# Feed-forward products with the high and low activations side by side in one moving operand of 512 columns

## Chip, cores and metric

The kernel runs on one core of one Trainium2 chip. The metric is the device time of one execution in microseconds; the number for the kernel before is the median of 3 runs.

## What is computed

Two transformer layers in float32 on 256 tokens of width 1024. Each ends in a feed-forward block: normalize, multiply by a 1024 x 4096 matrix, relu, square, multiply by a 4096 x 1024 matrix, add to the residual stream. The change touches these two blocks; attention, convolution and gates before them stay as they are.

```python
def rms_norm(x, g):
    xf = x.astype(jnp.float32)
    y = xf * lax.rsqrt(jnp.mean(xf * xf, axis=-1, keepdims=True) + EPS)
    return (y * g.astype(jnp.float32)).astype(x.dtype)

# end of the first layer (hybrid_layer); D_MODEL 1024, D_FF 4096, SEQ 256
    h = rms_norm(x, norm2_g)
    return x + jnp.square(jax.nn.relu(h @ w_up)) @ w_down
...
# end of the second layer (second_block)
        hf = _rmsnorm(h, norm_ffn_g[l]) @ w_ff1[l]
        h = h + jnp.square(jax.nn.relu(hf)) @ w_ff2[l]
    return _rmsnorm(h, norm_final_g)
```

## The kernel before

**Products.** A float32 operand is written as the sum of a high part, rounded to the type fp32r, and a low part, the remainder. A product is then high weights x high activations, high weights x low activations, and low weights x high activations (`mm3`, L258, its matmuls at L264, L266 and L268). Weights are the stationary operand (128 x 128), activations the moving one: 128 rows of one contraction tile k and all 256 tokens. A `Feat` (class at L270) is a group that makes four output tiles o of 128 features: its two PSUM tiles `ps[0]` and `ps[1]` (half b = 0 and 1) hold two output tiles of 256 columns each, one bank a half. The pool `psm` has four such banks, so two groups can be open at once.

**Order.** A unit of weights is 1 MB: four contraction tiles by four output tiles. `chunk(c)` takes the next unit and issues its 16 x 3 matmuls. In the last chunk of a group the matmuls of half 0 come first, then its eviction `evac`, then those of half 1, then its eviction; in the others both halves alternate. `prod` (L375) runs groups one behind the other, or two in turns (`pair`). TensorE's instructions run in the order of the program (it is in `MANUAL`). Those of ScalarE and VectorE are sorted before the run by a planner, which follows what it takes to be ready and, among ready ones, program order, lifted for side work.

**Weights.** `Stream.next` loads units ahead and splits the one that is needed two units later in two pieces: ScalarE rounds the high part (L123, 128 x 1024), VectorE subtracts for the low part (L126). A split needs buffers of a unit that is used up.

**The up product** (`ffn_up`): 8 groups g of 8 contraction tiles, so two units each; the first two groups are a pair. Eviction of a half: ScalarE takes the relu from PSUM (L929), VectorE squares in SBUF (L930), then `split_into` makes the high part on ScalarE (L396) and the low part on VectorE (L397) in a `Split`, where one tile holds high and low parts of two contraction tiles beside each other.

**The down product.** In the first layer it is `residual` with 32 contraction tiles: two Feat groups of eight units, one behind the other. Eviction: VectorE scales from PSUM (L867), adds to the residual stream x (L868), ScalarE squares it (L873), VectorE adds the squares up (L880, L882). `add_up` puts the column sums of the squares on TensorE (L436) one call of `pump` later, that is in the midst of the next group's first unit; the next normalization hangs on them. In the second layer the down product is a `Tok` group: activations stationary, weights moving, 512 columns (L355 to L357).

`pump` is called twice in each chunk and issues a piece of side work (normalization sums, transposes, the memory's loading).

Of the kernel before, what the change touches and what calls it, by code (L numbers as in the profile page):

```python
# [9 lines left out]
F32 = mybir.dt.float32  # L10
# [6 lines left out]
T = 256  # L17
# [38 lines left out]
class Split:  # L56
# [11 lines left out]

    def lo(self, k, n=1):
        return self._part(1, k, n)  # L70

    def _part(self, h, k, n):
        t = self.tiles[k // 2]
# [87 lines left out]
def hybrid_conformer_kernel(ctx, tc, stop, dbg, xT, memT, wall, wtok, wkiwi, wcmp, par_d, cst_d, gfin_d, out):  # L161
# [3 lines left out]
    const = ctx.enter_context(tc.tile_pool(name="const", bufs=1))  # L165
    half = ctx.enter_context(tc.tile_pool(name="half", bufs=H_BUFS))
    sm = ctx.enter_context(tc.tile_pool(name="sm", bufs=2))
    psm = ctx.enter_context(tc.tile_pool(name="psm", bufs=4, space=bass.MemoryType.PSUM))
    pss = ctx.enter_context(tc.tile_pool(name="pss", bufs=3, space=bass.MemoryType.PSUM))
    pso = ctx.enter_context(tc.tile_pool(name="pso", bufs=1, space=bass.MemoryType.PSUM))  # L170

# [19 lines left out]

    def PS(name="s"):
        return pss.tile([128, 512], F32, name=name, tag="s")

    def bc(ap, n):
        return ap.unsqueeze(1).to_broadcast([128, n, ap.shape[-1]])
# [18 lines left out]
    def v4(ap):  # L215
        return ap.rearrange("p n (s a) -> p n s a", s=2)
# [40 lines left out]

    ALL8 = list(range(8))  # L258

    def mm3(ps_ap, wh, wl, xh, xl, first, last, part=None):  # L260
        ps_ap = ps_ap.rearrange("p (a s) -> p a s", s=2)
        xh, xl = turns(xh), turns(xl)
        if part in (None, 0):
            P.matmul(out=ps_ap, lhsT=wh, rhs=xh, start=first, stop=False, skip_group_check=True)  # L264
        if part in (None, 1):
            P.matmul(out=ps_ap, lhsT=wh, rhs=xl, start=False, stop=False, skip_group_check=True)  # L266
        if part in (None, 2):
            P.matmul(out=ps_ap, lhsT=wl, rhs=xh, start=False, stop=last, skip_group_check=True)  # L268

    class Feat:  # L270


        def __init__(self, act, kts, evac, kmajor=False):
            self.act, self.kts, self.evac, self.kmajor = act, kts, evac, kmajor
            self.nch = len(kts) // 4
            self.ps = None

        def chunk(self, c):
            if self.ps is None:
                self.ps = [psm.tile([128, 2, T], F32, name="m", tag="m") for _ in range(2)]  # L280
            ps, act = self.ps, self.act
            wh, wl = W.next()
            wh = wh.rearrange("p (k o) -> p k o", k=4)
            if wl is not None:
                wl = wl.rearrange("p (k o) -> p k o", k=4)
            ks = self.kts[4 * c:4 * c + 4]
            end = c == self.nch - 1

            def one(kk, o, part=None):
                k = ks[kk]  # L290
                sl = slice(o * 128, o * 128 + 128)
                first = c == 0 and kk == 0 and o % 2 == 0
                last = end and kk == 3
                if wl is None:
                    P.matmul(out=plain(ps[o // 2])[:, o % 2], lhsT=wh[:, kk, sl], rhs=v3(act.raw(k)), start=first, stop=last, skip_group_check=True)  # L295
                else:
                    mm3(ps[o // 2][:, o % 2], wh[:, kk, sl], wl[:, kk, sl], act.hi(k), act.lo(k), first, last, part)

            if not end or self.kmajor:
                for kk in range(4):  # L300

                    for part in range(3) if self.kmajor and wl is not None else (None,):
                        for o in range(4):
                            one(kk, o, part)
                    if kk == 1:
                        pump()
                if end:
                    for b in range(2):
                        self.evac(plain(ps[b]), 2 * b, 2)
            else:  # L310
                for b in range(2):
                    for kk in range(4):
                        for o in (2 * b, 2 * b + 1):
                            one(kk, o)
                    self.evac(plain(ps[b]), 2 * b, 2)
                    if b == 0:
                        pump()
            pump()

    class Tok:  # L320
# [10 lines left out]
        def chunks(self, c, num, mid=None):  # L331

            if self.ps is None:
                self.ps = [psm.tile([128, 512], F32, name="m", tag="m") for _ in range(2)]
            ps, act, n = self.ps, self.act, self.n
            ws = []
            for _ in range(num):
# [44 lines left out]
                for c in range(g.nch):  # L382
                    g.chunk(c)

    def group(act, kts, evac, kmajor=False):
        prod([Feat(act, kts, evac, kmajor)])

    def tok_group(act, kts, n, evac):
        prod([Tok(act, kts, n, evac)])
# [93 lines left out]
    with tc.manual_schedule(engines=MANUAL):  # L483
# [3 lines left out]
        with tc.manual_schedule(engines={mybir.EngineType.Activation}):  # L487
            nc.scalar.dma_start(out=par0, in_=par_d[:, 0:8])
            A.activation(out=S([128, 1], "tab"), in_=ones[:, 0:1], func=AF.Exp)
        warm = psm.tile([128, 2, T], F32, name="m", tag="m")  # L490
        for i in range(WARM):
            P.matmul(out=warm[:, i % 2, 0:128], lhsT=ones, rhs=ones)
        x = B8(name="x")
# [361 lines left out]

        prod([ba(0), ba(1)])

        def residual(act, kts, x, sp, gname, scale_b=None, kmajor=False, pair=True, stats=None):

            def one(hf):  # L860
                def ev(ps, o, n):
# [25 lines left out]

                        later.append((STATS_LAG, add_up))

                return Feat(act, kts, ev, kmajor=kmajor and hf == 0)  # L890

            prod([one(0), one(1)], pair=pair)

# [4 lines left out]
        def ffn_up(act, src, tagr, bcast):  # L898
            res = {}

            def norm_side():
                for _ in range(9):
                    yield
                s = sq_sum(src, "s")
                for _ in range(5):
                    yield
                ps = col_stats(s)
                r = rstd_col(ps, D, "r" + tagr)
                r2 = const.tile([128, 2], F32, name="rsq" + tagr)
                V.tensor_tensor(r2, r, r, op=ALU.mult)  # L910
                res["col"] = r2
                if not bcast:
                    return
                dg = col_diag(r2)
                yield
                ps = diag_bcast(dg)
                rb = S([128, T], "rb", 4)
                A.activation(out=rb, in_=ps, func=AF.Copy)
                res["b"] = rb

            res["gen"] = start(norm_side())
            hs = Split([])
            gs = []
            for g in range(8):
                hs.tiles += HL("hh", 4).tiles

                def ev(ps, o, n, g=g):
                    r = S([128, 2, T], "pr", PR_BUFS)
                    A.activation(out=v4(r), in_=ps, func=AF.Relu)  # L929
                    V.tensor_tensor(r, r, r, op=ALU.mult)  # L930
                    split_into(hs, r, n, 4 * g + o)

                gs.append(Feat(act, ALL8, ev))
            prod(gs[:2], pair=True)
            prod(gs[2:])
            return hs, res
# [40 lines left out]
        mems, mem_steps, mem_sum = load_mem()  # L977
        msd = start(mem_side())
        st3 = {}
        residual(hs, list(range(32)), x, None, None, scale_b=res["b"], pair=False, stats=st3)  # L980
        drain(msd)
        dump2("x3", x)
        if stop == 1:
# [45 lines left out]
        def heads_pv(pt, nb, v, h0, sp, tt, pool=None):  # L1029

            if pool is psm:
                po = psm.tile([128, 2, T], F32, name="m", tag="m").rearrange("p a t -> p (a t)")
            else:
                po = PS() if pool is pss else pso.tile([128, 512], F32, name="o", tag="o")
            for r in range(2):
# [162 lines left out]
        for hf in range(2):  # L1198
# [19 lines left out]

            group(xs2, ALL8, ev_qi)
            kiwi = S([128, T], "rb", 4)  # L1220
            ps = psm.tile([128, 2, T], F32, name="m", tag="m")
            wh, wl = W.next()
            for k in range(8):
                sl = slice(128 * k, 128 * k + 128)
# [300 lines left out]
```

## Time and profile before

| | |
|---|---|
| median of 3 runs (lowest, highest) | 895.32 us (895.29, 895.41) |
| the profiled execution's own time, its span | 895.22 us, 893.4 us |
| TensorE matmuls, busy | 881.9 us, 99% of the span, 7240 instructions |
| VectorE | 659.8 us, 74% |
| ScalarE | 545.4 us, 61% |
| GpSimd | 18.6 us, 2% |
| HBM read | 162.58 MB, 183 GB/s over the span |

All numbers of the trace are of one profiled execution. A matmul's row is longer than its distance from the next, since matmuls overlap in the pipeline; the pace is read from start to start in the timeline. PE is TensorE's matmul, DVE VectorE, ACT ScalarE; L12 is line 12 of the kernel. In names like `m<-fh,wh` the output comes first; `m` are the accumulators of `psm`, `wh` and `wl` the high and low parts of the weights, `hh` the tiles of the up product's result (high and low), `fh` those of its input. In the first layer the up product takes 231 to 318 us and the down product 318 to 404.6 us; in the second layer they take 715.5 to 803.4 and 803.4 to 886.5 us.

### The profile page before, as it was taken

To read this page: it belongs to the slowest core of one execution; us is meant where nothing else is said; L and a number is where in the kernel's file an instruction comes from. 1 tells how busy PE (TensorE), PEld (TensorE's weight loads), DVE (VectorE), ACT (ScalarE), POOL (GpSimd) and SP (SyncE) were. 2 spreads that over 40 slices of the span, in tenths; PEclk is the share of its full clock that TensorE was granted. 3 is DMA by queue.
4 is the path that set the end of the run, shared out by engine and by line. 5 is a ranking of instruction groups with operands and counts; after the bars stand their busy time and mean duration, and the time that the engine had idled before them with its cause. 6 is when DMAs were issued, how large, how long until landed. Compare 5 with 4: busy or idle time off the path is not lost.

```text
span 893.4 us, 17269 instructions
## 1 busy us (share of the span) xinstructions
PE 881.9 (99%) x7240; PEld 852.8 (95%) x7240; DVE 659.8 (74%) x1037; ACT 545.4 (61%) x925; POOL 18.6 (2%) x21
## 2 busy tenths in 40 slices
PE   9999999999999999999999999999999999999996
PEld 8999999999999999999998989999999999998885
DVE  6678899457787675648699999997787777665542
ACT  7634667444575564434697799977566657554432
POOL 0121000000000000000000000000000000000000
PEclk9999999999999999999999999999999999999999
DMA  8944623455555566554553356354565265555531
GB/s 305 313 161 146 222 98 140 158 211 198 190 190 189 192 241 219 197 189 140 186 209 107 139 193 236 112 192 166 199 250 203 104 216 189 190 202 209 198 142 48
DMA packets 25566, 165.01 MB, mean 185 GB/s; under 512 B 2960, under 2 KB 3600, under 8 KB 6928
## 3 DMA queue, kind: packets, MB, share of 16 engines
q1 hardware_dynamic: 25056, 163.37, 51.8%
q8 instruction: 57, 0.93, 0.4%
q10 hardware_dynamic: 432, 0.53, 0.2%
q14 instruction: 21, 0.17, 0.1%
HBM read 162.58 MB, written 1.05 MB: 183 GB/s over the span
## 4 chain that ended last, share of the span: by engine, by line
PE 89%; DVE 5%; ACT 2%; issue 1%; DMA 1%; POOL 1%; POOLq 0%; DVEq 0%
PE m L264 23%; PE m L266 23%; PE m L268 23%; PE m L355 4%; PE m L356 4%; PE m L357 4%; DVE wl L126 2%; PE m L295 2%; DMA wr<-in_wall_dram 1%; PE m L352 1%; DVE y L1147 1%; PE o L785 1%; PE s L769 1%; PE s L1065 1%; POOL coqk L631 1%
## 5 line engine op out<-in xcount | busy, mean ns | idle before, releaser
L126 DVE TENSOR_TENSOR wl<-wr,wh 128x1024 fp32r<-128x1024 f32 (+2 forms) x300 | 350.4, 1191 | 155.2 <-ACT wh L123 154.8
L123 ACT ACTIVATE wh<-wr 128x1024 fp32r<-128x1024 f32 (+2 forms) x300 | 298.5, 1028 | 204.2 <-PE m L266 95.9
L264 PE MATMUL m<-xnh,wh 128*128 128x256 f32 x376 | 106.6, 283 | 0.0
L266 PE MATMUL m<-xnh,wh 128*128 128x256 f32 x376 | 103.4, 275 | 0.0
L268 PE MATMUL m<-xnh,wl 128*128 128x256 f32 x376 | 103.4, 275 | 0.0
L264 PE MATMUL m<-xh,wh 128*128 128x256 f32 x384 | 100.5, 282 | 0.9 <-ACT xh L523 0.9
L266 PE MATMUL m<-xh,wh 128*128 128x256 f32 x384 | 98.0, 276 | 0.0
L268 PE MATMUL m<-xh,wl 128*128 128x256 f32 x384 | 97.8, 275 | 0.0
L1146 ACT ACTIVATE cp<-u,par 128x255 f32<-128x255 f32 (+23 forms) x192 | 78.8, 492 | 0.0
L266 PEld LDWEIGHTS m<-xnh,wh 128*128 128x128 f32 x376 | 72.2, 192 | 0.7 <-issue 0.5
L264 PEld LDWEIGHTS m<-xnh,wh 128*128 128x128 f32 x376 | 72.2, 192 | 0.7 <-issue 0.5
L264 PEld LDWEIGHTS m<-xh,wh 128*128 128x128 f32 x384 | 69.8, 192 | 2.8 <-issue 1.4
L268 PEld LDWEIGHTS m<-xnh,wl 128*128 128x128 f32 x376 | 72.2, 192 | 0.0
L264 PE MATMUL m<-x5h,wh 128*128 128x256 f32 x256 | 70.8, 277 | 0.0
L264 PE MATMUL m<-fh,wh 128*128 128x256 f32 x256 | 70.6, 276 | 0.0
L264 PE MATMUL m<-hh,wh 128*128 128x256 f32 x256 | 70.6, 276 | 0.0
L268 PE MATMUL m<-x5h,wl 128*128 128x256 f32 x256 | 70.4, 275 | 0.0
L266 PE MATMUL m<-fh,wh 128*128 128x256 f32 x256 | 70.4, 275 | 0.0
L268 PE MATMUL m<-fh,wl 128*128 128x256 f32 x256 | 70.4, 275 | 0.0
L266 PE MATMUL m<-hh,wh 128*128 128x256 f32 x256 | 70.4, 275 | 0.0
L268 PE MATMUL m<-hh,wl 128*128 128x256 f32 x256 | 70.4, 275 | 0.0
L266 PE MATMUL m<-x5h,wh 128*128 128x256 f32 x256 | 70.4, 275 | 0.0
(380 smaller groups left out, 2318.1 us busy)
## 6 DMA issues: line engine op xcount, KB each, us to landing
wr<-in_wall_dram SPq DMA_DIRECT2D x145, 1024.0 KB, 4.9
wr<-in_wall_dram SPq DMA_DIRECT2D x4, 512.0 KB, 9.1
mem<-in_memT_dram SPq DMA_DIRECT2D x4, 512.0 KB, 5.8
wr<-in_wtok_dram SPq DMA_DIRECT2D x2, 560.0 KB, 5.5
wr<-in_wall_dram SPq DMA_DIRECT2D x4, 256.0 KB, 5.1
wck<-in_wcmp_dram SPq DMA_DIRECT2D x2, 512.0 KB, 8.6
cst<-in_cst_dram SPq DMA_DIRECT2D x1, 776.0 KB, 10.7
x<-in_xT_dram SPq DMA_DIRECT2D x2, 256.0 KB, 4.2
```

Source lines behind the costliest of these rows:

```text
L123: self.nc.scalar.activation(out=hi[:, sl], in_=raw[:, sl], func=AF.Copy)
L126: self.nc.vector.tensor_sub(lo[:, sl], raw[:, sl], hi[:, sl].bitcast(F32))
L264: P.matmul(out=ps_ap, lhsT=wh, rhs=xh, start=first, stop=False, skip_group_check=True)
L266: P.matmul(out=ps_ap, lhsT=wh, rhs=xl, start=False, stop=False, skip_group_check=True)
L268: P.matmul(out=ps_ap, lhsT=wl, rhs=xh, start=False, stop=last, skip_group_check=True)
L295: P.matmul(out=plain(ps[o // 2])[:, o % 2], lhsT=wh[:, kk, sl], rhs=v3(act.raw(k)), start=first, stop=last, skip_group_check=True)
L352: P.matmul(out=o.rearrange("p a s -> p s a"), lhsT=act.raw(k)[:, tk], rhs=wh[:, w], start=first, stop=last)
L355: P.matmul(out=o, lhsT=xh, rhs=wh[:, w], start=first, stop=False)
L356: P.matmul(out=o, lhsT=xh, rhs=wl[:, w], start=False, stop=False)
L357: P.matmul(out=o, lhsT=xl, rhs=wh[:, w], start=False, stop=last)
L631: G.tensor_tensor(co, ms, mhalf, op=ALU.pow)
L1146: A.activation(out=p[:, i, 0:T - d], in_=u[hf][:, i, 0:T - d], func=AF.Copy, scale=w[i])
```

## The change

In groups g = 2 to 7 of both up products and in both groups of the first layer's down product (`wide`), a contraction tile's high and low activations, which already lie in one tile, become one moving operand of 512 columns against the high weights; a second matmul of 256 columns multiplies low weights by high activations onto the first 256 of these. An output tile's accumulator is then a whole bank, the low activations' product in its second half. A PSUM tile of `psm` is now two banks and the pool has two of them (`PM`), so a wide half takes one tile, a wide group both; a group that isn't wide has both its halves in one tile. In a wide chunk all matmuls of half 0 come before those of half 1. The eviction of a wide half has ScalarE copy the second halves to SBUF and VectorE add the first halves to them; after that the old eviction goes on from SBUF, in the up product with relu and square as one VectorE instruction (max with 0, times itself).

```diff
+    def both(self, k):
+        return self.tiles[k // 2][:, :, k % 2]
...
-    psm = ctx.enter_context(tc.tile_pool(name="psm", bufs=4, space=bass.MemoryType.PSUM))
+    psm = ctx.enter_context(tc.tile_pool(name="psm", bufs=2, space=bass.MemoryType.PSUM))
...
+    def PM():
+
+        return psm.tile([128, 2, 2, T], F32, name="m", tag="m")
...
+    def mm2(ps_ap, wh, wl, xhl, first, last):
+
+        P.matmul(out=ps_ap.rearrange("p h (a s) -> p h a s", s=2), lhsT=wh, rhs=xhl.rearrange("p h (s a) -> p h a s", s=2),
+                 start=first, stop=False, skip_group_check=True)
+        P.matmul(out=ps_ap[:, 0].rearrange("p (a s) -> p a s", s=2), lhsT=wl, rhs=turns(xhl[:, 0]), start=False, stop=last,
+                 skip_group_check=True)
...
-        def __init__(self, act, kts, evac, kmajor=False):
-            self.act, self.kts, self.evac, self.kmajor = act, kts, evac, kmajor
+        def __init__(self, act, kts, evac, kmajor=False, wide=False):
+            self.act, self.kts, self.evac, self.kmajor, self.wide = act, kts, evac, kmajor, wide
...
+        def chunk_wide(self, c):
+
+            if self.ps is None:
+                self.ps = [None, None]
+            wh, wl = (w.rearrange("p (k o) -> p k o", k=4) for w in W.next())
+            ks = self.kts[4 * c:4 * c + 4]
+            end = c == self.nch - 1
+            for b in range(2):
+                if c == 0:
+                    self.ps[b] = PM()
+                m = self.ps[b]
+                for kk in range(4):
+                    for o in range(2):
+                        sl = slice((2 * b + o) * 128, (2 * b + o) * 128 + 128)
+                        mm2(m[:, o], wh[:, kk, sl], wl[:, kk, sl], self.act.both(ks[kk]), c == 0 and kk == 0, end and kk == 3)
+                if end:
+                    t = S([128, 2, T], "pr", PR_BUFS)
+                    A.activation(out=v4(t), in_=plain(m[:, :, 1]), func=AF.Copy)
+                    V.tensor_tensor(v4(t), plain(m[:, :, 0]), v4(t), op=ALU.add)
+                    self.evac(v4(t), 2 * b, 2)
+                pump()
+
         def chunk(self, c):
+            if self.wide:
+                self.chunk_wide(c)
+                return
             if self.ps is None:
-                self.ps = [psm.tile([128, 2, T], F32, name="m", tag="m") for _ in range(2)]
+                m = PM()
+                self.ps = [m[:, 0], m[:, 1]]
...
-        def residual(act, kts, x, sp, gname, scale_b=None, kmajor=False, pair=True, stats=None):
+        def residual(act, kts, x, sp, gname, scale_b=None, kmajor=False, pair=True, stats=None, wide=False):
...
-                    A.activation(out=v4(r), in_=ps, func=AF.Relu)
-                    V.tensor_tensor(r, r, r, op=ALU.mult)
+                    if g < 2:
+                        A.activation(out=v4(r), in_=ps, func=AF.Relu)
+                        V.tensor_tensor(r, r, r, op=ALU.mult)
+                    else:
+                        V.scalar_tensor_tensor(out=v4(r), in0=ps, scalar=0.0, in1=ps, op0=ALU.max, op1=ALU.mult)
                     split_into(hs, r, n, 4 * g + o)
 
-                gs.append(Feat(act, ALL8, ev))
+                gs.append(Feat(act, ALL8, ev, wide=g > 1))
...
-        residual(hs, list(range(32)), x, None, None, scale_b=res["b"], pair=False, stats=st3)
+        residual(hs, list(range(32)), x, None, None, scale_b=res["b"], pair=False, stats=st3, wide=True)
```

## Rows read from the trace of the kernel before

A timeline row is: start us, us, engine, line, operation, output<-input, shapes, count; in brackets how long the engine sat idle before it, and what released it.

**Rows 1.** Stages: start:end, length, then busy us (x instructions) of each engine

```profile
231.00:318.00 87.00, 87.00 (x781) 87.00 (x780) 61.77 (x76) 53.16 (x69) 1.08 (x1) 1.00 0.57 196
...
318.00:404.60 86.60, 86.60 (x778) 86.60 (x777) 49.89 (x57) 40.21 (x48) 0.70 (x1) 1.00 0.58 207
```

**Rows 2.** TensorE's waits over the whole run: us in total, times, longest

```profile
PE s L1164 <- DVE ys L1161: 1.1, 1, 1.1
...
PE s L436 <- ACT pr L873: 0.2, 1, 0.2
```

**Rows 3.** Timeline of TensorE, first down product, 256 columns; first and last of 38

```profile
359.78 0.28 PE L266 MATMUL m<-hh,wh 128*128 128x256 f32 x1
...
363.91 0.28 PE L268 MATMUL m<-hh,wl 128*128 128x256 f32 x1
```

**Rows 4.** Timeline of TensorE, second down product, 512 columns; first and last of 21

```profile
829.65 0.38 PE L356 MATMUL m<-wl,hh 128*128 128x512 f32 x1
...
833.97 0.38 PE L355 MATMUL m<-wh,hh 128*128 128x512 f32 x1
```

**Rows 5.** Timeline of TensorE, token product of 280 columns; first and last of 16

```profile
31.40 0.28 PE L356 MATMUL m<-wl,xh 128*128 128x280 f32 x1
...
33.19 0.28 PE L356 MATMUL m<-wl,xh 128*128 128x280 f32 x1
```

**Rows 6.** Timeline of ScalarE and VectorE, first up product, middle of a group

```profile
302.13 2.02 ACT L123 ACTIVATE wh<-wr 128x1024 fp32r<-128x1024 f32 x2 [1.77 <-PE m L266]
...
303.23 2.36 DVE L126 TENSOR_TENSOR wl<-wr,wh 128x1024 fp32r<-128x1024 f32 x2 [1.79 <-ACT wh L123]
...
305.56 0.69 DVE L930 TENSOR_TENSOR pr<-pr 128x512 f32<-128x512 f32 x1
...
306.28 0.63 ACT L396 ACTIVATE hh<-pr 128x512 fp32r<-128x512 f32 x1 [0.76 <-DVE pr L930]
```

**Rows 7.** Timeline of TensorE: the first matmul of a group, three boundaries

```profile
263.63 0.28 PE L264 MATMUL m<-fh,wh 128*128 128x256 f32 x1
...
275.16 0.36 PE L264 MATMUL m<-fh,wh 128*128 128x256 f32 x1
...
318.12 0.28 PE L264 MATMUL m<-hh,wh 128*128 128x256 f32 x1
```

**Rows 8.** Timeline of ScalarE at two of these boundaries

```profile
263.64 0.63 ACT L396 ACTIVATE hh<-pr 128x512 fp32r<-128x512 f32 x1 [1.89 <-DVE pr L930]
...
264.18 1.04 ACT L123 ACTIVATE wh<-wr 128x1024 fp32r<-128x1024 f32 x1
...
318.21 1.06 ACT L123 ACTIVATE wh<-wr 128x1024 fp32r<-128x1024 f32 x1 [0.58 <-PE m L266]
...
319.18 0.58 ACT L929 ACTIVATE pr<-m 128x512 f32<-128x512 f32 x1
```

**Rows 9.** Timeline of VectorE at the three boundaries

```profile
266.39 0.69 DVE L930 TENSOR_TENSOR pr<-pr 128x512 f32<-128x512 f32 x1
...
278.35 0.69 DVE L930 TENSOR_TENSOR pr<-pr 128x512 f32<-128x512 f32 x1
...
319.31 1.23 DVE L126 TENSOR_TENSOR wl<-wr,wh 128x1024 fp32r<-128x1024 f32 x1 [0.95 <-ACT wh L123]
...
320.45 0.69 DVE L930 TENSOR_TENSOR pr<-pr 128x512 f32<-128x512 f32 x1
```

**Rows 10.** Timeline of VectorE, end of the first down product

```profile
402.88 0.68 DVE L867 TENSOR_TENSOR pr<-m,rb 128x512 f32<-128x512 f32 x1
...
403.60 0.69 DVE L868 TENSOR_TENSOR x<-pr,x 128x512 f32<-128x512 f32 x1
```

**Rows 11.** Timeline of TensorE behind the first down product, column sums in it

```profile
404.78 0.28 PE L264 MATMUL m<-memh,wh 128*128 128x256 f32 x1
...
407.46 0.28 PE L436 MATMUL s<-ones,pr 128*128 128x1 f32 x2
...
407.93 1.28 PE L436 MATMUL s<-ones,pr 128*128 128x1 f32 x10 [0.19 <-ACT pr L873]
```

More of the change, by code (lines that the diff above doesn't have):

```diff
@@ L333, in chunks @@
             if self.ps is None:
-                self.ps = [psm.tile([128, 512], F32, name="m", tag="m") for _ in range(2)]
+                m = PM().rearrange("p b a t -> p b (a t)")
+                self.ps = [m[:, 0], m[:, 1]]
             ps, act, n = self.ps, self.act, self.n
@@ L383, in prod, with group @@
                     g.chunk(c)
-    def group(act, kts, evac, kmajor=False):
-        prod([Feat(act, kts, evac, kmajor)])
+    def group(act, kts, evac, kmajor=False, wide=False):
+        prod([Feat(act, kts, evac, kmajor, wide)])
     def tok_group(act, kts, n, evac):
@@ L489, in hybrid_conformer_kernel @@
             A.activation(out=S([128, 1], "tab"), in_=ones[:, 0:1], func=AF.Exp)
-        warm = psm.tile([128, 2, T], F32, name="m", tag="m")
+        warm = PM()[:, 0]
         for i in range(WARM):
@@ L888, in ev @@
                         later.append((STATS_LAG, add_up))
-                return Feat(act, kts, ev, kmajor=kmajor and hf == 0)
+                return Feat(act, kts, ev, kmajor=kmajor and hf == 0, wide=wide)
             prod([one(0), one(1)], pair=pair)
@@ L1031, in heads_pv @@
             if pool is psm:
-                po = psm.tile([128, 2, T], F32, name="m", tag="m").rearrange("p a t -> p (a t)")
+                po = PM()[:, 0].rearrange("p a t -> p (a t)")
             else:
@@ L1220, in hybrid_conformer_kernel @@
             kiwi = S([128, T], "rb", 4)
-            ps = psm.tile([128, 2, T], F32, name="m", tag="m")
+            ps = PM()[:, 0]
             wh, wl = W.next()
```

## The prediction

> **What bounds the kernel now.** I read the page's engine shares first (the table above), then busy time by stage [rows 1], then TensorE's waits [rows 2], and then the timeline. TensorE is at work 99% of the span, at the full clock. In the first up product (231 to 318 us) and the first down product (318 to 404.6 us) it is busy for every microsecond, while VectorE has 61.8 of 87.0 us and ScalarE 53.2 [rows 1]. The longest wait of TensorE on another engine in the whole run is 1.1 us, and only one of its waits lies in the stages that change, 0.2 us for the squares after the down product [rows 2]. So in these stages the time is the number of matmuls times their pace. A product becomes faster only by a shorter matmul sequence, and any new wait of TensorE adds to the end at once, because TensorE runs in the written order with nothing to put in between.
>
> The pace is the distance from start to start, not the 275 ns of a row, for the rows overlap. At 256 columns: 37 steps from 359.78 to 363.91 us, 0.1116 us each [rows 3]. At 512 columns: 20 steps from 829.65 to 833.97 us, 0.216 us each [rows 4]. At 280 columns: 15 steps in 1.79 us, 0.1193 us [rows 5].
>
> **What the change saves.** A step (one contraction tile k, one output tile o) is today three matmuls of 256 columns: 3 x 0.1116 = 0.3348 us. After it, it is one of 512 and one of 256: 0.216 + 0.1116 = 0.3276 us. That is 0.0072 us for each step. Steps: two up products with 6 wide groups of 8 k x 4 o, 384, and the first down product with 2 halves of 32 k x 4 o, 256; 640 in all, so 640 x 0.0072 = 4.6 us. Upper bound: the 256-column pace stands 0.002 us above the line through 280 and 512 columns, which falls by 0.00042 us a column to 0.1093 at 256. If the matmul that stays ran on that line (a third of the weight loads is gone), a step would cost 0.3253 us and the saving be 6.1 us. I take 4.6, since the row for 256 columns is the nearest one, and keep 6.1 for the range.
>
> The Trainium skill ("TensorE: Matmul & The Clock Gate", Back-to-back issue gap) gives N / 2.4 + 2.5 ns for a warm matmul. The 512-column row agrees (215.8 ns against 216), the 256-column row doesn't (109.2 against 111.6); by the page the saving would be an estimated 6.3 us in place of 4.6.
>
> **What it adds: the evictions.** A wide group needs 2 banks for each half b (two output tiles), 4 for both: all the banks of this pool. So where before the next group began in other banks, now its half b must wait until the same half of the group before has been read out. And the reading is longer: ScalarE copies the low sums, then VectorE adds the high sums from PSUM; only then are the banks free. Before, one ScalarE instruction (Relu) freed them. The relu and square that follow are one VectorE instruction on SBUF, so ScalarE's count per eviction stays at two, and VectorE's goes from two to three. That is at most 0.75 us more in a group of 10.5 us, where VectorE has 71% now [rows 1]: capacity is left, and I cost it at nothing while weight pieces stay ahead; order within the queue is what costs.
>
> How long a half has: 8 steps of the other half, 8 x 0.3276 = 2.62 us.
>
> Half 0 is read out in the middle of a unit of weights. There ScalarE begins the unit's two weight pieces at 302.13, VectorE works at theirs from 303.23, and the first VectorE instruction of the eviction starts at 305.56 [rows 6]. Put the add there: it is done at 306.25, 4.1 us after the unit began, and needed 5.24 us after it (16 steps). No wait.
>
> Half 1 ends with the group, and there the next unit's pieces are released at the same moment. The queues show the order: next group's first matmul at 318.12 [rows 7], weight piece on ScalarE at 318.21, only then the eviction's read at 319.18 [rows 8], on VectorE the piece's low part at 319.31, then the eviction's instruction at 320.45, 0.69 us long [rows 9]. The piece goes first because its high part is free one matmul before the sums are complete. With the add in the place of that instruction, the banks are free at 321.14, 3.02 us after the boundary; needed at 2.62. TensorE waits 0.40 us. It can be more: the half-0 chain is now longer (add, then relu-square, each some 0.7 us, before ScalarE's high part of the result, which started at 306.28 [rows 6]). That high part moves to about 307.05, some 0.2 us before the boundary, and holds ScalarE for 0.54 us. At 263.63 such a row stands across a boundary already: the piece starts at 264.18 in place of 263.72, and the VectorE instruction ends at 267.08, 3.45 us after [rows 7 to 9], a wait of 0.83 us. It also tells the order: both the piece and the eviction were ready at 264.18, and the piece came first. I take 0.5 us between the ends 0.40 and 0.83.
>
> How often: the half-1 banks are taken over from a wide eviction five times in each up product and once by the down product's first half, 11 x 0.5 = 5.5 us (4.4 to 9.1). The second down half takes over from the first, with VectorE otherwise idle: 0.4 us. Where side work stands in the queues it is worse: at the boundary of 275.16 the VectorE instruction starts at 278.35 and ends 3.88 us after [rows 7, 9], a wait of 1.26; a like one, with the transposes, is in the second up product. I add 0.8 us (0 to 1.6) for the two together.
>
> The second down product keeps its form and takes the banks over with two units in between: nothing.
>
> **What it moves: the statistics after the down product.** TensorE has the column sums of the squares in its written order 2.68 us after the last down matmul (404.78 to 407.46), and waits there already, up to 407.93 [rows 11]. They hang on a serial VectorE chain that begins at 402.88, when the weight pieces are done [rows 10]. The change puts an add into it for each half, paced 0.65 (0.72 where the next instruction needs the result, 402.88 to 403.60 [rows 10]): 1.3 us. A weight piece of 1.15 us can slip in as well, since the low copy queues on ScalarE behind it: 2.8 us at most with its ScalarE share. All of it lands on TensorE, which is waiting already. I take 1.9 (1.3 to 2.8).
>
> **The sum.** -4.6 + 5.5 + 0.4 + 0.8 + 1.9 = +4.0 us on the profiled execution of 895.22 us (span 893.4 and 1.8 around it); the median of the runs shown is 0.1 above it. Forecast 899.3 us. Its own range: low ends -6.1 + 4.4 + 0.4 + 0 + 1.3 = 0.0, high ends -4.6 + 9.1 + 0.4 + 1.6 + 2.8 = +9.3.
>
> **Rivals.** (1) Faster: at a boundary the eviction goes ahead of the weight piece. One mechanism: the planner picks whatever is ready when ScalarE comes free. If in its plan the half-0 high part starts before the piece is released (0.09 us after the boundary) and ends after the sums are complete (0.2 us after), both are ready and the older one, the eviction, is first. My own estimate, -0.2 to +0.32 us, lies in that window; against it stands the row at 264.18, where the same overlap gave the piece first. The banks are then free about 1.7 us after a boundary, no wait in the up products, and -4.6 to -6.1 + 0.4 + 1.3 to 1.9 gives -2.3 to -4.4: 892 us. (2) They cancel: boundary waits of 0.3 us or less, as when pieces are split earlier: within 1.8 us of before, 895.5. (3) Worse: the high part comes late, after the piece, and the eviction after both; a further 0.55 us of ScalarE and 0.6 of VectorE at each boundary, so waits of 1.0 to 1.4 us and 904 to 908. (4) That the 512-column matmul isn't at its pace because its two halves lie apart in SBUF: the 512-column rows read a spread pattern too [rows 4], so I give it almost nothing, inside (3).
>
> The Trainium skill ("Trainium Kernel Development and Optimization", Best Practices) says that consistent bubbles can mean that PSUM ran out. No such bubble stands in these stages now; the forecast is that it would appear at every wide boundary.
>
> **How the numbers follow.** Forecast 0.42, rival 1 0.33, rival 2 0.16, rival 3 with 4 0.09. A measurement of this kernel can tell about 0.2%, 1.8 us, from no change. The forecast's range has a small share below that, so slower 0.47, within 0.2% 0.19, faster 0.34. The range that leaves out 2 in 10 goes from 891.0 (rival 1) to 904.5; the forecast's own is 895.2 to 904.5.
>
> **What would show it.** Saving: 512 and 256 alternating at 0.216 and 0.11 us; right if a step is 0.325 to 0.328. Boundary waits: in the list of waits TensorE waits for VectorE's add some 12 times, 0.4 to 0.8 us each, at half 1, never at half 0. If these rows are absent and ScalarE's copy precedes the weight piece, rival 1 holds. Statistics: the sums' wait grows from 0.2 us to about 2. I am wrong if the 256-column matmul in the mixture is much quicker than 0.109, or if the queues are sorted otherwise at the boundaries.

## The result and the profile after

| | before | after |
|---|---|---|
| median | 895.34 us (4 runs) | 1012.86 us (4 runs, 1010.04 to 1013.64) |
| the profiled execution, its span | 895.22, 893.4 us | 1013.49, 1011.7 us |
| ratio | | 1.131, 95% interval 1.128 to 1.133 |

The change makes the kernel 13% slower. The forecast was 899.3 us with a range to 904.5: the direction was right, the size was short by 114 us, and the time lies far outside the range.

First the page of the kernel after, engine shares (busy us, share of the span, instructions) and, by 40 slices, TensorE's share and its granted clock in tenths:

```profile
span 1011.7 us, 16034 instructions
...
PE 916.7 (91%) x6600; PEld 858.4 (85%) x6600; DVE 685.8 (68%) x1065; ACT 549.6 (54%) x929; POOL 17.0 (2%) x21
...
PE   9879889987899999995998998998988989999996
...
PEclk9888999999999999997999999999899999999999
```

The granted clock before, from the page of that kernel:

```profile
PEclk9999999999999999999999999999999999999999
```

TensorE has 640 matmuls fewer and is busy 35 us longer: 91% of a longer span in place of 99%. Its share has dents everywhere, not only in the slices of the feed-forward products, and the clock, which was at 9 in every slice, has dents as well (mean 0.967 in place of 0.998). Its waits on other engines (us in total, times, longest) say where; the head of that list and the two rows that the forecast was about:

```profile
PE m L278 <- DVE x L905: 11.1, 5, 3.2
PE m L278 <- DVE cs L843: 7.4, 2, 6.0
PE m L278 <- DVE km L1056: 6.5, 1, 6.5
PE m L278 <- DVE y L861: 6.0, 2, 4.3
...
PE m L269 <- DVE pr L310: 4.9, 10, 1.2
...
PE s L477 <- ACT pr L914: 2.6, 1, 2.6
...
PE s L477 <- DVE pr L923: 1.2, 1, 1.2
```

The whole list sums to 88 us; before it was 4.5, with 1.1 us as the longest [rows 2]. L278 is the first matmul of an ordinary step, which the change didn't touch; what it waits for are evictions of the convolution branch (L843, L861), the residual products (L905), the memory's keys (L1056). The wide steps (L269) have 4.9 us of it, the statistics (L477) 3.8. So nearly all of the loss is in products that kept their form.

One of these waits, in the timeline of an ordinary group, TensorE and ScalarE:

```profile
564.10 0.28 PE L282 MATMUL m<-xnh,wl 128*128 128x256 f32 x1
564.41 0.60 ACT L1277 ACTIVATE q<-m 128x512 f32<-128x512 f32 x1 [5.53 <-PE m L282]
565.06 0.38 PE L278 MATMUL m<-xnh,wh 128*128 128x256 f32 x1 [0.69 <-ACT q L1277]
565.27 0.28 PE L280 MATMUL m<-xnh,wh 128*128 128x256 f32 x1
```

564.10 is the last matmul of half 0 of a group of queries, 565.06 the first of half 1 of the same group. Between them ScalarE reads half 0 out (564.41 to 565.01), and only then does TensorE go on: 0.96 us from start to start where 0.11 was usual. Half 1 writes to another bank than the one that is read, but since the change both halves lie in one tile (`PM`), and the program now has a wait there. Where VectorE does the eviction and has other work queued, as with `cs` (that queue waits for GpSimd until 55.66 us, and small work and two weight pieces follow before the eviction at 58.96), one such wait takes 6.0 us.

### The profile page after: what moved, and what is told of

It reads as the page before. It is cut to its first block, busy times and chain, and to the rows that moved or that the text cites. A ratio compares the mean times of both kernels' runs of the same rounds, so it can differ in the third digit from the quotient of the medians.

```text
span 1011.7 us, 16034 instructions
## 1 busy us (share of the span) xinstructions
PE 916.7 (91%) x6600; PEld 858.4 (85%) x6600; DVE 685.8 (68%) x1065; ACT 549.6 (54%) x929; POOL 17.0 (2%) x21
## 4 chain that ended last, share of the span: by engine, by line
PE 66%; DVE 18%; ACT 9%; issue 4%; DMA 2%; POOL 1%; POOLq 0%; ACTq 0%; DVEq 0%
PE m L269 12%; PE m L278 12%; PE m L280 10%; PE m L282 10%; DVE wl L129 9%; PE m L271 6%; ACT wh L126 5%; PE m L396 3%; PE m L397 3%; PE m L398 3%; PE m L335 2%; DMA wr<-in_wall_dram 2%; ACT cp L1190 1%; PE m L393 1%; DVE pr L310 1%
## 5 line engine op out<-in xcount | busy, mean ns | idle before, releaser
L126 ACT ACTIVATE wh<-wr 128x1024 fp32r<-128x1024 f32 (+2 forms) x300 | 298.1, 1028 | 265.1 <-PE m L280 103.0
L278 PE MATMUL m<-xh,wh 128*128 128x256 f32 x384 | 105.2, 294 | 17.8 <-DVE cs L843 7.4
L278 PE MATMUL m<-xnh,wh 128*128 128x256 f32 x376 | 107.8, 287 | 14.4 <-DVE u L228 5.3
L280 PE MATMUL m<-xh,wh 128*128 128x256 f32 x384 | 101.8, 285 | 0.0
L282 PE MATMUL m<-xh,wl 128*128 128x256 f32 x384 | 101.4, 284 | 0.0
L278 PEld LDWEIGHTS m<-xh,wh 128*128 128x128 f32 x384 | 73.9, 203 | 21.4 <-DVE cs L843 7.8
L278 PEld LDWEIGHTS m<-xnh,wh 128*128 128x128 f32 x376 | 72.8, 194 | 18.3 <-DVE u L228 6.4
L269 PE MATMUL m<-hh,wh 128*128 128x512 f32 x256 | 84.5, 383 | 0.7 <-DVE pr L310 0.7
L280 PEld LDWEIGHTS m<-xh,wh 128*128 128x128 f32 x384 | 73.6, 202 | 0.4 <-DVE xh L566 0.4
L282 PEld LDWEIGHTS m<-xh,wl 128*128 128x128 f32 x384 | 73.5, 202 | 0.0
L269 PE MATMUL m<-fh,wh 128*128 128x512 f32 x192 | 63.8, 385 | 2.5 <-DVE pr L310 2.5
L269 PE MATMUL m<-x5h,wh 128*128 128x512 f32 x192 | 64.1, 386 | 1.7 <-DVE pr L310 1.7
L1191 DVE TENSOR_TENSOR y<-y,cp 128x1020 f32<-128x1020 f32 (+23 forms) x48 | 55.6, 1158 | 14.5 <-ACT cp L1190 13.1
L269 PEld LDWEIGHTS m<-hh,wh 128*128 128x128 f32 x256 | 48.4, 189 | 8.0 <-DVE pr L310 1.3
L271 PE MATMUL m<-fh,wl 128*128 128x256 f32 x192 | 52.3, 273 | 0.0
```

What stands on the lines that cost most here:

```text
L126: self.nc.scalar.activation(out=hi[:, sl], in_=raw[:, sl], func=AF.Copy)
L269: P.matmul(out=ps_ap.rearrange("p h (a s) -> p h a s", s=2), lhsT=wh, rhs=xhl.rearrange("p h (s a) -> p h a s", s=2), start=first, stop=Fa ...
L271: P.matmul(out=ps_ap[:, 0].rearrange("p (a s) -> p a s", s=2), lhsT=wl, rhs=turns(xhl[:, 0]), start=False, stop=last, skip_group_check=True)
L1191: V.tensor_tensor(y[hf][:, :, d:T], y[hf][:, :, d:T], p[:, :, 0:T - d], op=ALU.add)
```

## The experiments

**Only the tiles.** The change without wide products: tiles of two banks, two of them, the relu and square of before.

```diff
-                    if g < 2:
+                    if True:
...
-                gs.append(Feat(act, ALL8, ev, wide=g > 1))
+                gs.append(Feat(act, ALL8, ev, wide=False))
...
-        residual(hs, list(range(32)), x, None, None, scale_b=res["b"], pair=False, stats=st3, wide=True)
+        residual(hs, list(range(32)), x, None, None, scale_b=res["b"], pair=False, stats=st3)
```

> Only the accumulators change: tiles of two banks, two of them, both halves of a group in one tile; no wide product, the old relu and square. Theory (the matmuls of half 1 wait until half 0 of their own group has been read out, because both lie in one tile): the waits of the changed kernel's ordinary groups stand here too, and the 14 groups of the feed-forward products that are no longer wide get one each, 0.8 to 1.5 us; 1005 to 1035 us. Rival (the wide groups upset the order of ScalarE and VectorE for the rest of the program): without them the loss is gone, under 915 us.

Measured: 1015.52 us (ratio 1.134, 1.131 to 1.137). TensorE's waits, the same list:

```profile
PE m L278 <- ACT pr L971: 12.8, 16, 1.8
PE m L278 <- DVE x L905: 11.1, 5, 3.2
PE m L278 <- DVE cs L843: 7.4, 2, 6.0
PE m L278 <- DVE km L1056: 6.5, 1, 6.5
```

The rows of L905, L843 and L1056 are those of the kernel after to the tenth, without one wide matmul in the program. At L971, the relu of ordinary up groups, the kernel after has 4 waits with 4.1 us, for the two groups of each up product that stayed ordinary; here all eight groups of each are ordinary, and it has 16 waits. The allocation alone is enough for the loss.

**Reading late.** The kernel after, but ordinary groups and token groups read both halves out when half 1 is through.

```diff
                             one(kk, o)
-                    self.evac(plain(ps[b]), 2 * b, 2)
                     if b == 0:
                         pump()
+                for b in range(2):
+                    self.evac(plain(ps[b]), 2 * b, 2)
...
+                    if tt == 0:
+                        pump()
+                for tt in range(2):
                     self.evac(ps[tt][:, :n], tt)
-                    if mid is None or tt == 0:
-                        pump()
+                if mid is None:
+                    pump()
```

> The changed kernel, but ordinary groups (and token groups) read both halves out after the last matmul of half 1. Theory (half 1's matmuls wait for half 0's reading): no such wait is left, since nothing is read before half 1 is through; the next group has the other tile; 898 to 915 us. Rival (two tiles in place of four are too few, groups wait for the reading of earlier groups): reading later makes it worse, over 1013 us.

Measured: 918.86 us (1.026, 1.024 to 1.028), 94 us less than the kernel after. The head of its list of waits:

```profile
PE m L269 <- DVE pr L310: 5.5, 12, 1.2
PE s L481 <- ACT pr L918: 2.6, 1, 2.6
PE s L1085 <- ACT vm L1348: 2.6, 1, 2.6
```

No ordinary matmul waits for an eviction any more. So it isn't that two tiles are too few, for then later reading would have made it worse: half 1 was waiting for the reading of its own half 0. What is left at the head are the waits of the forecast (L269, twelve of them; L481, the statistics) and such as L1085, where cross attention waits for its values (`vm`), which are now read out later: from the first matmul of its queries to the last of its output product the timeline has 49.7 us in place of 41.3, which is more than the 4 us by which this kernel lies over the expected upper end.

**One-bank tiles.** The change as forecast, without the shared tile: four tiles of one bank as before, a wide half takes two of them.

```diff
-    psm = ctx.enter_context(tc.tile_pool(name="psm", bufs=2, space=bass.MemoryType.PSUM))
+    psm = ctx.enter_context(tc.tile_pool(name="psm", bufs=4, space=bass.MemoryType.PSUM))
...
-        return psm.tile([128, 2, 2, T], F32, name="m", tag="m")
+        return psm.tile([128, 2, T], F32, name="m", tag="m")
...
-                    self.ps[b] = PM()
+                    self.ps[b] = [PM(), PM()]
...
-                    A.activation(out=v4(t), in_=plain(m[:, :, 1]), func=AF.Copy)
-                    V.tensor_tensor(v4(t), plain(m[:, :, 0]), v4(t), op=ALU.add)
+                    for o in range(2):
+                        A.activation(out=v3(t[:, o]), in_=plain(m[o])[:, 1], func=AF.Copy)
+                        V.tensor_tensor(v3(t[:, o]), plain(m[o])[:, 0], v3(t[:, o]), op=ALU.add)
...
-                m = PM()
-                self.ps = [m[:, 0], m[:, 1]]
+                self.ps = [PM(), PM()]
...
```

> The changed kernel with accumulator tiles of one bank, four of them, as before; a wide half takes two of them, and its eviction is two copies and two adds of 256 columns. Theory (all of the loss beyond the forecast is the shared tile): ordinary groups wait as little as before the change; left are the saving of 4.6 us, waits at the boundaries of wide groups of at most 0.45 us each (12 of them) and the statistics' 2 to 3 us: 893 to 901 us. Rival (the wide products or their heavier evictions cost it): over 930 us.

Measured: 900.52 us (1.0056, 1.0039 to 1.0073). Of the 117.5 us, 112.3 go with the shared tile (1012.86 less 900.52); some 3.6 of these are boundary waits of wide groups, which fall from 4.9 to 1.3 us here. The profiled execution has a span of 898.4, 5.0 over that of before, and by first and last matmul of each product in the timeline this lies so:

| product | before, us | one-bank tiles, us |
|---|---|---|
| first up product | 86.5 | 86.7 |
| first down product | 86.6 | 85.0 |
| memory group behind it | 12.7 | 19.7 |
| from there to the second up product | 297.9 | 298.5 |
| second up product | 87.8 | 87.0 |
| second down product | 82.7 | 82.7 |

So the products that were changed are quicker by 2.2 us together, and the memory group, which wasn't, takes 7.0 more. There, in the waits, the timeline of TensorE, and two stretches by engine (start:end, length, then busy us of PE, PEld, DVE, ACT, POOL, granted clock, DMA share, GB/s):

```profile
PE s L476 <- ACT pr L913: 3.1, 1, 3.1
PE m L269 <- DVE pr L311: 1.3, 1, 1.3
...
PE s L476 <- DVE pr L922: 0.9, 1, 0.9
```

```profile
406.64 0.38 PE L476 MATMUL s<-ones,pr 128*128 128x1 f32 x2 [0.89 <-DVE pr L922]
...
410.09 2.30 PE L476 MATMUL s<-ones,pr 128*128 128x1 f32 x10 [3.07 <-ACT pr L913]
...
414.10 0.42 PE L282 MATMUL m<-memh,wl 128*128 128x256 f32 x1
...
416.01 0.42 PE L282 MATMUL m<-memh,wl 128*128 128x256 f32 x1
```

```profile
412.00:416.00 4.00, 4.00 (x19) 4.00 (x20) 0.64 (x3) 0.00 (x0) 1.34 (x3) 0.50 0.04 14
416.00:423.00 7.00, 7.00 (x64) 7.00 (x63) 4.83 (x10) 3.54 (x5) 0.00 (x0) 0.98 0.01 2
```

The column sums wait 0.9 and 3.1 us for their squares. Behind the longer wait the ten small matmuls take 2.30 us where they took 1.28 [rows 11], and from 412 to 416 us TensorE is busy throughout at a granted clock of 0.50, the lower of its two levels, 1.2 GHz: nine steps of 256 columns from 414.10 to 416.01, 0.212 us each in place of 0.1116 [rows 3]. That is about 1.0 + 1.9 us on top of the wait. By the same view the clock is at 0.50 from 409.5 us, while TensorE still waits, to 416.3.

The boundary waits are almost gone in this kernel: one, 1.3 us, where the norm's side work stands in the queues. ScalarE at a boundary:

```profile
307.12 0.63 ACT L436 ACTIVATE hh<-pr 128x512 fp32r<-128x512 f32 x1 [1.81 <-DVE pr L973]
307.66 0.65 ACT L310 ACTIVATE pr<-m 128x256 f32<-128x256 f32 x2
308.19 2.01 ACT L126 ACTIVATE wh<-wr 128x1024 fp32r<-128x1024 f32 x2
```

The eviction's copies (L310) stand ahead of the weight pieces (L126), right behind the high part of half 0 (L436): the order of the first rival. Besides, a tile is free after its own copy and add, so TensorE can begin with the first output tile of a half while the second is still read. Which of the two does more here wasn't separated.

**Low weights first.** One-bank tiles, and in each wide step the 256-column matmul ahead of the one of 512.

```diff
-        P.matmul(out=ps_ap.rearrange("p h (a s) -> p h a s", s=2), lhsT=wh, rhs=xhl.rearrange("p h (s a) -> p h a s", s=2),
-                 start=first, stop=False, skip_group_check=True)
-        P.matmul(out=ps_ap[:, 0].rearrange("p (a s) -> p a s", s=2), lhsT=wl, rhs=turns(xhl[:, 0]), start=False, stop=last,
-                 skip_group_check=True)
+        P.matmul(out=ps_ap[:, 0].rearrange("p (a s) -> p a s", s=2), lhsT=wl, rhs=turns(xhl[:, 0]), start=first, stop=False,
+                 skip_group_check=True)
+        P.matmul(out=ps_ap.rearrange("p h (a s) -> p h a s", s=2), lhsT=wh, rhs=xhl.rearrange("p h (s a) -> p h a s", s=2),
+                 start=False, stop=last, skip_group_check=True)
```

> As the one with one-bank tiles, but in each step the low weights' matmul comes first and the one of 512 columns last, so that the high weights come free no earlier than the sums are complete. Theory of the boundary waits (the weight piece goes ahead of the eviction because it is ready one matmul earlier): the copies now come ahead of the pieces, the waits at half 1 are gone, 1 to 4 us faster than with the old order. Rival (the waits come from VectorE's share of the work, not from the order): no change.

Measured: 900.84 us (1.0063, 1.0048 to 1.0078), no difference from 900.52. The 1 to 4 us that were expected didn't come, and this doesn't decide what it was meant to decide: with one-bank tiles there was but one boundary wait to remove, and it has another reason. The same edit belongs where the waits stand:

**Low weights first, two-bank tiles, reading late.** The diff of the late reading and this one together:

```diff
-        P.matmul(out=ps_ap.rearrange("p h (a s) -> p h a s", s=2), lhsT=wh, rhs=xhl.rearrange("p h (s a) -> p h a s", s=2),
-                 start=first, stop=False, skip_group_check=True)
-        P.matmul(out=ps_ap[:, 0].rearrange("p (a s) -> p a s", s=2), lhsT=wl, rhs=turns(xhl[:, 0]), start=False, stop=last,
-                 skip_group_check=True)
+        P.matmul(out=ps_ap[:, 0].rearrange("p (a s) -> p a s", s=2), lhsT=wl, rhs=turns(xhl[:, 0]), start=first, stop=False,
+                 skip_group_check=True)
+        P.matmul(out=ps_ap.rearrange("p h (a s) -> p h a s", s=2), lhsT=wh, rhs=xhl.rearrange("p h (s a) -> p h a s", s=2),
+                 start=False, stop=last, skip_group_check=True)
...
-                    self.evac(plain(ps[b]), 2 * b, 2)
...
+                for b in range(2):
+                    self.evac(plain(ps[b]), 2 * b, 2)
...
```

> The kernel with tiles of two banks and the late eviction of ordinary groups (918.9 us), with the low weights' matmul first and the one of 512 columns last in each wide step. There the waits at half 1 stand (0.43 us each, some ten of them, 5.5 us in all). Theory (a weight piece is ready one matmul before the sums and so goes ahead of the eviction on ScalarE): the copy now comes before the piece and most of these waits go, 912 to 916 us. Rival (the reading simply takes longer than the 2.62 us, whatever the order): waits stay at 4 us or more and the time within 1 us.

Measured: 912.3 us (1.0191, 1.0166 to 1.0215), against 918.86 in the old order. ScalarE at the start of the fifth wide group of the first up product, first in the kernel after (old order; with late reading the same three stand in the same order there), then in this one:

```profile
345.57 0.63 ACT L437 ACTIVATE hh<-pr 128x512 fp32r<-128x512 f32 x1 [1.48 <-DVE pr L974]
346.10 1.04 ACT L126 ACTIVATE wh<-wr 128x1024 fp32r<-128x1024 f32 x1
347.05 0.58 ACT L309 ACTIVATE pr<-m 128x512 f32<-128x512 f32 x1
```

```profile
297.23 0.63 ACT L441 ACTIVATE hh<-pr 128x512 fp32r<-128x512 f32 x1 [1.59 <-DVE pr L978]
297.77 0.58 ACT L309 ACTIVATE pr<-m 128x512 f32<-128x512 f32 x1
298.24 1.99 ACT L126 ACTIVATE wh<-wr 128x1024 fp32r<-128x1024 f32 x2
```

In the old order: high part of the result (L437), weight piece (L126), then the eviction's copy (L309). In the new one the copy comes right behind the high part and both pieces after it. TensorE's waits for the add fall from 5.5 us in 12 to 2.2 in 3, those at half 1 from ten to one:

```profile
PE m L269 <- DVE pr L310: 2.2, 3, 1.2
```

The three wide products are together 5.7 us shorter in the traces (first to last matmul), more than the 3.3 us of idle time: a wait costs more than the idle time in its row, as the section on the forecast shows. So the boundary waits at half 1 come from the order on ScalarE, as the forecast had it, and with two-bank tiles the order from what is ready one matmul earlier.

**Second half of the down product ordinary.** One-bank tiles; only the first half is wide, so the chain to the column sums is the one of before.

```diff
-                return Feat(act, kts, ev, kmajor=kmajor and hf == 0, wide=wide)
+                return Feat(act, kts, ev, kmajor=kmajor and hf == 0, wide=wide and hf == 0)
```

> The kernel with one-bank tiles (900.5 us), but of the down product only the first half is wide; the second is ordinary, so the chain to the column sums of squares is that of the kernel before. Theory (7 us of that kernel's loss lie in the memory group behind the down product: 4.0 us of waiting for the sums and 3 us of a lower clock after it): 900.5 - 7.0 + 128 x 0.0072 = 894.4 us, 893 to 895.3, and the granted clock there back at 1.00. Rival (the wait comes from VectorE's fuller queue in general): at most 2 us better.

Measured: 893.9 us (11 runs; 0.9984, 0.9976 to 0.9993), 6.6 less than with both halves wide, and as the only version below the kernel before, by 1.4 us or 0.16%. The memory group takes 12.7 us again; in the waits and the stretch of the sums:

```profile
PE s L476 <- ACT pr L913: 0.2, 1, 0.2
```

```profile
402.00:412.00 10.00, 9.81 (x89) 9.73 (x88) 8.30 (x13) 3.74 (x5) 1.26 (x3) 1.00 0.47 146
```

The sums wait 0.2 us, as before [rows 2], at a clock of 1.00. (Its profiled execution, 895.69 us, is the slowest of its eleven runs; it has 1.9 us of waiting at the start of the program.)

**Sums one pump later.** One-bank tiles, both halves wide.

```diff
-STATS_LAG = 1
+STATS_LAG = 2
```

> The kernel with one-bank tiles and the whole down product wide, with the column sums put on TensorE one pump later (5.4 in place of 2.7 us after the down product). Theory: the squares come 7 us after it, so the wait shrinks from 4.0 to about 1.5 us and the clock stays up, but the normalization that hangs on the sums is then late at the end of the memory group by 1 to 2 us: 896 to 898 us. Rival (the clock falls for another reason than this wait): the slow stretch stays, over 899 us.

Measured: 895.32 us (10 runs; 1.000, 0.9991 to 1.001), 5.2 less:

```profile
PE s L476 <- ACT pr L913: 1.6, 1, 1.6
```

The wait is 1.6 us, the memory group 15.7 in place of 19.7, and the time 0.7 us under the expected range. The clock didn't stay up, though. In the page of this run it is at 9 in every slice, but a slice is 22 us long; the stretch behind the sums and two matmuls in it:

```profile
412.00:415.40 3.40, 3.40 (x18) 3.40 (x18) 1.76 (x4) 0.00 (x0) 1.35 (x3) 0.51 0.22 92
```

```profile
412.36 0.42 PE L278 MATMUL m<-memh,wh 128*128 128x256 f32 x1
...
414.06 0.42 PE L282 MATMUL m<-memh,wl 128*128 128x256 f32 x1
```

Eight steps in 1.70 us, 0.212 us each: the lower clock stands here for 3.4 us, where it stood for 6.8 with the sums one pump earlier. The 3.0 us by which the group is still longer than before are the longer wait, 1.4 us (from the first sums to the others 1.84 us in place of 0.47 [rows 11]), and about 1.6 us of lower clock, so the late normalization cost nothing that can be seen. The low stretch shrinks with the wait for the sums: 6.8 us with waits of 4.0, 3.4 with 1.6, none with 0.2 (before, and with the second half ordinary). The 7.0 us of the memory group are thus the chain to the sums, with the clock behind it. The length of the wait alone isn't shown to be the reason: in this same kernel the boundary wait of 1.3 us in the up product leaves the clock at 1.00 (270 to 300 us).

## Why the forecast was wrong

**The step that failed** is in "What it adds: the evictions": it follows the banks of wide groups only, and of the rest it says that the second down product "keeps its form and takes the banks over with two units in between: nothing". The tiles of all ordinary groups changed, and they weren't costed. I asked whether a group finds its banks free when it begins, and it does; I didn't ask what happens inside a group that has two halves in one tile, the first of which is read out while the second is still being written. The case stands in the text of the change itself: a group that isn't wide has both its halves in one tile. Even the second down product, which was named and put at nothing, waits for the reading of its own first half, 1.6 and 1.0 us:

```profile
PE m L396 <- DVE x5t L1426: 1.6, 1, 1.6
...
PE m L396 <- DVE x5t L1433: 1.0, 1, 1.0
```

The price of this step is nearly all of the 112.3 us by which one-bank tiles are quicker (3.6 are boundary waits, as said). The waits in groups that aren't wide make some 75 us (88 less 4.5 as before, 4.9 at wide boundaries and 3.8 for the statistics). Each also costs more than the idle time in its row: in the group of queries shown, 1.17 us from the last matmul of half 0 to the second of half 1 (564.10 to 565.27) in place of 0.22, with 0.69 idle, so 0.26 more. To this comes a lower clock, 0.967 on the mean against 0.994 with one-bank tiles. By the two pages TensorE is idle 78.0 us longer than in the one-bank kernel (1011.7 less 916.7, against 898.4 less 881.4) and busy 35.3 us longer for the same 6600 matmuls. How these 35.3 divide between the clock and the matmuls behind a wait wasn't separated.

Without it the forecast's sum can be held against the one-bank kernel and the boundaries of the kernel after:

- **Saving.** Right in the pace of a step; the sum of the products shows a little less. In the kernel after, timeline of TensorE in wide groups; at 300.86 and 311.34 the first matmuls of two groups:

```profile
300.86 0.38 PE L269 MATMUL m<-fh,wh 128*128 128x512 f32 x1
...
311.34 0.38 PE L269 MATMUL m<-fh,wh 128*128 128x512 f32 x1
...
338.31 0.38 PE L269 MATMUL m<-fh,wh 128*128 128x512 f32 x1
338.53 0.27 PE L271 MATMUL m<-fh,wl 128*128 128x256 f32 x1
```

  32 steps from 300.86 to 311.34, 0.3275 us each; 0.3276 was worked out, with the 256-column matmul at its old pace. With one-bank tiles the first down product is 1.6 us shorter, of 1.8 for its 256 steps, and the second up product 0.8, of 1.4; in the first up product the one wait takes back the 1.4. So some 0.8 us of the 4.6 aren't found, and where they stay is open. The 6.3 us that the prediction gives by the Trainium skill ("TensorE: Matmul & The Clock Gate", Back-to-back issue gap) are wrongly worked out: they set the formula's step after (325.0 ns) against the measured step before (334.8). With the formula on both sides the step before is 327.5 ns and the saving an estimated 1.6 us; the measured steps, 334.8 and 327.5 ns, lie above it both times.
- **Boundary waits.** Right in cause and cost where two-bank tiles stand, not wholly in place. The kernel after, VectorE's add and TensorE:

```profile
345.85 0.38 PE L269 MATMUL m<-fh,wh 128*128 128x512 f32 x1
...
348.32 0.68 DVE L310 TENSOR_TENSOR pr<-m,pr 128x512 f32<-128x512 f32 x1
348.36 0.27 PE L271 MATMUL m<-fh,wl 128*128 128x256 f32 x1
...
349.06 0.48 PE L269 MATMUL m<-fh,wh 128*128 128x512 f32 x1 [0.43 <-DVE pr L310]
...
357.02 0.38 PE L269 MATMUL m<-fh,wh 128*128 128x512 f32 x1
```

  The add ends at 349.00 and half 1 begins at 349.06, with 0.43 us of idle time. What the wait costs is more: this group takes 11.17 us to the next one's first matmul (345.85 to 357.02), the one without a wait 10.48, so 0.69 us; 0.40 to 0.83 was given and 0.5 taken. With reading late there are 12 such waits with 5.5 us of idle time, by the same 0.26 us on top of each an estimated 8.6 us; 5.5 + 0.4 + 0.8 = 6.7 was given. "Never at half 0" doesn't hold: one of the ten waits of the kernel after stands there (0.39 us, behind a group with other matmuls in it), and two of the twelve with reading late (0.48 and 0.39).
- **Statistics.** Right in place, too small: 1.3 to 2.8 us was the range, with one-bank tiles it is 4.0 - 0.2 = 3.8 us of waiting and 3 us of lower clock. The weight piece slipped into the chain, as the upper end had it, and not one piece but two (in the timeline of VectorE one stands before the adds, one before the scaling); and that the clock falls with such a wait wasn't in the sum at all. The kernel after has the same: waits of 1.2 and 2.6 us, and a clock of 0.50 from 463 to 467 us.
- **Rivals.** Eviction ahead of the piece is what the one-bank kernels and the low-first order show, and it does remove these waits. That the 512-column matmul would be slow is ruled out (0.3275 us a step). None of the four held the wait that made the loss.

The forecast of 899.3 is close to the 900.5 us of one-bank tiles, but that agreement is in part luck: boundary waits of 1.3 us (1.5 with what follows them) in place of 6.7, the memory group's 7.0 in place of 1.9.

Left open: why the wait between two banks of one tile is written into the program. The runs show that it is, and before the change TensorE writes one tile's bank while ScalarE reads another's: the read at 319.18 stands amid the matmuls that begin at 318.12 [rows 7, 8].

## What to carry to other kernels

In this program a tile is also the unit in which waits are made: when two buffers that are filled and emptied one after the other are put into one tile, the filling of the second waits for the emptying of the first, in every user of the pool, so a change of a shared pool is to be followed through all its users and inside each group, not only at the take-over. A matmul product that is bound by TensorE gains by fewer, longer matmuls only what the pace rows say, 2% of a step here; a single chain behind it whose waits became 3.8 us longer took 7.0 here, more than all of it. Where weight pieces and evictions share an engine, as here on ScalarE, the order of the last two matmuls can decide which of them is ready first. And a mean over slices of 22 us can hide a low clock of 3.4 us; the starts of the matmuls show it.

## What the runs showed of the hardware

TensorE's granted clock, at 9 in every slice of the page before, fell to 0.50 (1.2 GHz) in the one-bank kernel during the 3.1 us wait for the statistics, at 409.5 us, and stood there to 416.3, though TensorE was at work again from 410.09; it is 0.98 in the stretch from 416 to 423 us. Matmuls of 256 columns took 0.212 us there, 0.1116 at the full clock. With a wait of 1.6 us in its place the clock was 0.51 from 412.0 to 415.4 us, with 0.2 us it stayed at 1.00, and a 1.3 us wait in the up product left it at 1.00. In the kernel after, with 60 waits of up to 6.5 us, the mean clock was 0.967.

A wait of TensorE costs more than the idle time in its row: 0.69 us for 0.43 in a wide group, and 0.26 us more than the idle time in the group of queries, both with the clock at 1.00. A matmul of 512 columns whose halves lie 2 KB apart runs at the pace of the second down product's, whose 512 columns lie in one stretch: 0.3275 us a step is 0.216 [rows 4] and 0.1116, so the 256-column pace stays too when every second matmul is one of 512.
